# Score matmuls of 128 columns instead of 256 for the first query block of a sliding-window head

## The chip, the cores and the metric

The kernel runs on one core of one Trainium2 chip. The metric is the device time of one execution in microseconds (us). Before the change three runs took 303.61, 304.22 and 304.19 us; their median is 304.19 us. Beside them one execution was recorded by the hardware profiler; it took 303.86 us.

## The reference, cut to what matters

One decoder layer on a sequence of 512 tokens with model width 1024: a normed and modulated input is projected to queries, keys, values and gates, attention is computed for two groups of eight heads (head dimension 64, two key/value heads in each group), the results are gated, projected back and added to the input. Group a is sliding-window attention with a window of 128 keys, a relative bias and one sink per head. Group b has compressed, selected and windowed branches; the change does not touch it. Group a, in blocks of 128 queries:

```python
# query t attends keys s with 0 <= t - s < window; window = 128, blocks of 128 queries
start = i * 128
kb = keys[start - 128 : start + 128]           # zero-padded in front of key 0
dist = t[:, None] - s[None, :]
mask = (dist >= 0) & (dist < 128) & (s >= 0)
logits = einsum('btgrd,bsgd->bgrts', q_block, kb) + bias
p = masked_softmax(logits, mask, sink)
o = einsum('bgrts,bsgd->btgrd', p, v_block)
```

For the blocks i = 1, 2, 3 there are 256 keys to score. For the first block, i = 0, only the 128 keys of the block itself exist.

## The kernel before, in words

**Precision and tiles.** Everything is float32 in memory. The large products run as float32r matmuls: each operand is split into a rounded high part and a low rest, and three products (high with high, high with low, low with high) are summed in PSUM. PE stands for TensorE, DVE for VectorE, ACT for ScalarE, POOL for GpSimd.

**Stages.** Up to about 60 us of the span the input is normed, modulated and projected to the queries, keys and values of group a (`first_proj`, lines 305 to 312, tiles `sq` and `skv`). Then two strands are woven together. One is a stream of projections, `gen1` and `gen2` (lines 818 and 877), whose matmuls stand at line 513 (`unit_nat`, 256 or 280 columns) and line 524 (`unit_col`, mostly 512 columns), all into tiles `pj`. The other is a list of attention slots, run by `run` (line 1032). Its first 16 slots are of kind a, four heads r by four query blocks i, with r outermost; kind b follows. After the last slots, the output projection runs through line 524 again.

**One slot.** A slot serves two heads at a time, one for each key/value head g. It goes through four steps in four successive turns of the loop in `run`:

- `slot_scores` (line 920): for each g two float32r matmuls at line 937, with the query block as the stationary operand (128 by 128, its high and low parts stacked in the 128 rows) and the keys as the moving operand, once their high and once their low part (`hl_`). Then DVE adds the bias and takes a row minimum at line 945 (the scores are negated), POOL copies the sink into a column at line 949, and ACT takes the exponential at line 952.
- `slot_scale` (line 956): divides by the row sum, one g on DVE (line 977), one on ACT (line 975).
- `slot_trans` (line 979): PE transposes the probabilities into tiles `pt` (line 988 for up to two key blocks, line 998 for more), ACT copies them out (line 989 or 999).
- `slot_pv` (line 1003): plain float32 matmuls with the values at line 1015, gathered for all four blocks of a head.

**Widths.** In `slot_scores`, `w` is the number of keys that count: 128 for kind a with i = 0, 256 for kind a with i = 1 to 3, and 256, 384 or 512 for the slots of kind b that reach this line. `n` is the number of key columns that the matmul streams. It is `max(w, 256)`, so that it differs from `w` only for kind a with i = 0. There the matmul also scores keys 128 to 255, and nothing reads those columns: line 945 takes `ps[g][:, 0:w]`.

**What sets the order.** DVE, ACT and PE each work through one list of instructions. The list is laid out when the program is built, not by the order of the source alone. `block()` (line 531) chains the PE instructions of attention steps to one another, so that they keep the order of the source among themselves; matmuls of the stream can be placed between them. How much of the stream is written between two attention steps is set by costs in us that the generators yield and by `PER_A` (line 31).

**Other matmuls that the prediction reads.** Line 248 (`mod_col`) multiplies a 128 by 128 stationary operand with one column. Line 677 (in `cmp_mlp`) multiplies a 128 by 128 stationary operand with 64 columns, line 644 a stationary operand of 64 columns with 256 columns; all three are plain float32, and in the profile each plain float32 matmul of the source appears as two MATMULs with a LDWEIGHTS each. A float32r matmul and a transpose appear as one of each.

Of the kernel before, what the change touches and what calls it, by code (L numbers as in the profile page):

```python
# [83 lines left out]
def hybrid_layer_kernel(ctx, tc, A, out):  # L84
# [817 lines left out]
    def slot_scores_both(sl, P):  # L902

        r = sl["id"][1]
        nm = sm.tile([128, 2, 2], F32, name="nm2", bufs=2)
        dn = sm.tile([128, 2, 2], F32, name="dn2", bufs=2)
        for g in range(2):
            ps = ps_s.tile([128, 512], F32, name="s")[:, 0:256].rearrange("p (b k) -> p b k", b=2)
            for hl_ in range(2):
                PE.matmul(ps, qs[8 + 4 * g + r][:, 0:128], kTb[g][:, :, hl_, 0:128], start=hl_ == 0, stop=hl_ == 1)  # L910
            for b in range(2):
                DVE.tensor_tensor_reduce(out=P[:, g, 128 * b:128 * b + 128], in0=ps[:, b], in1=bias["b", r, g][:, 384:512],
                                         scale=1.0, scalar=3e38, op0=OP.add, op1=OP.min, accum_out=nm[:, g, b:b + 1])
        for g in range(2):
            for b in range(2):
                v = P[:, g, 128 * b:128 * b + 128]
                ACT.activation(v, v, AF.Exp, bias=nm[:, g, b:b + 1], scale=-1.0, accum_out=dn[:, g, b:b + 1])
        sl.update(P=P, dn=dn, w=256, lo=0)

    def slot_scores(sl):  # L920
        kind, r, br, i = sl["id"]
        lo = max(0, i - 1) * 128 if kind == "a" else 0
        w = (i + 1) * 128 - lo
        P = mp.tile([128, 2, 257], F32, name="pa", bufs=3) if kind == "a" else mp.tile([128, 2, 512], F32, name="pp", bufs=3)
        if br == 3:
            slot_scores_both(sl, P)
            return
        nm = sm.tile([128, 2], F32, name="nm", bufs=4)
        dn = sm.tile([128, 2], F32, name="dn", bufs=4)
        ps_a = ps_s.tile([128, 512], F32, name="s") if kind == "a" else None  # L930
        ps = []
        for g in range(2):
            h = (0 if kind == "a" else 8) + 4 * g + r
            n = max(w, 256)
            ps.append(ps_a[:, 256 * g:256 * g + n] if kind == "a" else ps_s.tile([128, 512], F32, name="s")[:, 0:n])
            for hl_ in range(2):
                PE.matmul(ps[g], qs[h][:, 128 * i:128 * i + 128], kT[br, g][:, hl_, lo:lo + n], start=hl_ == 0,  # L937
                          stop=hl_ == 1)
        for g in range(2):
            h = (0 if kind == "a" else 8) + 4 * g + r  # L940
            if kind == "a":
                bt, init = bias["a", r][:, g, 256 - w:256], nsink[:, h:h + 1]
            else:
                bt, init = bias["b", r, g][:, 512 - w:512], 3e38
            DVE.tensor_tensor_reduce(out=P[:, g, 0:w], in0=ps[g][:, 0:w], in1=bt, scale=1.0, scalar=init,  # L945
                                     op0=OP.add, op1=OP.min, accum_out=nm[:, g:g + 1])
        e = w
        if kind == "a":
            POOL.tensor_copy(P[:, :, w:w + 1], nsink[:, r:8:4][:, :, None])
            e = w + 1  # L950
        for g in range(2):
            ACT.activation(P[:, g, 0:e], P[:, g, 0:e], AF.Exp, bias=nm[:, g:g + 1], scale=-1.0,  # L952
                           accum_out=dn[:, g:g + 1])
        sl.update(P=P, dn=dn, w=w, lo=lo)
# [77 lines left out]
    def run(slots, stream):  # L1032
# [3 lines left out]
        for t in range(n + 3):  # L1036
            per = PER_A if t < 16 else PER_B[t - 16 >= PER_B[2]]
            if t < n:
                kind, r, br, i = slots[t]["id"]
                if kind == "a" and i == 0 and r >= 2:  # L1040
                    load_bias_b(r - 2)
            if 0 <= t - 2 < n:
                with block():
                    slot_trans(slots[t - 2])
            if 0 <= t - 1 < n:
                slot_scale(slots[t - 1])
            if t < n:
                with block():
                    slot_scores(slots[t])
            stream.adv(per / 2)  # L1050
            if 0 <= t - 3 < n:
                group.append(slots[t - 3])
                kind, r, br, i = slots[t - 3]["id"]
                if i == NB - 1 and (kind == "a" or br == 2):
                    with block():
                        for sl in group:
                            slot_pv(sl)
                        if jobs:
                            jobs.pop(0)()
                            stream.debt += 3.6  # L1060
                    group = []
                    if kind == "b" and br == 2 and r + 2 < 4:
                        load_bias_b(r + 2)
            stream.adv(per / 2)
# [126 lines left out]
```

## Time and profile before

| | |
|---|---|
| median of 3 runs | 304.19 us (303.61 to 304.22) |
| profiled execution, its own time | 303.86 us |
| its span, first to last instruction | 301.8 us |
| time around the span | 2.1 us |
| granted TensorE clock, mean | 1.000 |
| PE busy | 295.1 us, 98% of the span |
| weight loads (PEld) busy | 251.9 us, 83% |
| DVE busy | 238.5 us, 79% |
| ACT busy | 195.9 us, 65% |
| POOL busy | 5.2 us, 2% |

In the profile, a group is named by line, engine and operation, then "output tile <- input tiles". PE is the matmul side of TensorE and PEld its weight load; the two overlap. Ends of matmuls are modelled, so the duration of one matmul (some 0.28 us for 256 columns) is longer than the distance from its start to the start of the next. This distance, the pitch, is what a matmul costs in a run of them. Where a view merges x4 equal instructions into one row, the row gives the time from the first start to the last end; the pitch is that time less one duration, divided by three.

### The profile page before, as it was taken

What the parts mean: (1) busy time and instruction counts of PE and PEld (TensorE: products, weight loads), DVE (VectorE), ACT (ScalarE), POOL (GpSimd) and SP (SyncE); (2) the same over time, 40 slices, a digit from 0 to 9 for tenths busy, and PEclk for the clock granted to TensorE, in tenths of its full rate; (3) what the DMA queues carried; (4) which work ended last, traced back from release to release, by engine and by line L of the source; (5) the groups of instructions that cost most, each with busy time, mean ns of one, the idle gap of its engine ahead of it and who ended that gap; (6) DMA issues with size and microseconds to landing.
All of it is one profiled execution on the core that took longest, in us unless ns stands there. A gap on an engine that the chain in (4) does not pass through costs nothing.

```text
span 301.8 us, 5849 instructions
## 1 busy us (share of the span) xinstructions
PE 295.1 (98%) x2118; PEld 251.9 (83%) x2119; DVE 238.5 (79%) x668; ACT 195.9 (65%) x474; POOL 5.2 (2%) x26
## 2 busy tenths in 40 slices
PE   8899999999999999999999999999999999999995
PEld 4677888889989999999786887798888888788885
DVE  3889996999995488878999999998986867727321
ACT  4876547767976478968696665866876875723100
POOL 1000000000100000000000000000000000000000
PEclk9999999999999999999999999999999999999999
DMA  7999957993285770320770022472130000005522
GB/s 274 370 383 405 362 188 256 261 266 136 74 206 176 228 230 2 106 71 0 262 261 3 2 95 98 157 275 72 34 109 2 0 2 1 2 0 169 181 70 72
DMA packets 27420, 44.21 MB, mean 147 GB/s; under 512 B 1712, under 2 KB 19408, under 8 KB 27392
## 3 DMA queue, kind: packets, MB, share of 16 engines
q1 hardware_dynamic: 27392, 43.84, 43.3%
q8 instruction: 17, 0.28, 0.4%
q14 instruction: 11, 0.09, 0.1%
HBM read 41.70 MB, written 2.14 MB: 145 GB/s over the span
## 4 chain that ended last, share of the span: by engine, by line
PE 80%; DVE 11%; ACT 5%; DMA 2%; issue 2%; SPq 0%; ACTq 0%; DVEq 0%
PE pj L524 30%; PE sq L310 8%; PE po L1015 8%; PE s L937 7%; PE pj L513 6%; PE pt L998 4%; PE skv L311 4%; PE pt L988 3%; PE s L644 2%; DMA xf<-in_xn 2%; DVE wl L192 2%; PE s L524 2%; DVE qs L577 2%; DVE pa L945 1%; ACT pa L952 1%
## 5 line engine op out<-in xcount | busy, mean ns | idle before, releaser
L191 ACT ACTIVATE wh<-raw 128x512 fp32r<-128x512 f32 (+1 forms) x52 | 31.7, 632 | 18.7 <-PE pj L524 16.0
L192 DVE TENSOR_TENSOR wl<-raw,wh 128x512 fp32r<-128x512 f32 (+1 forms) x52 | 35.1, 692 | 3.7 <-ACT wh L191 1.8
L513 PE MATMUL pj<-wl,hh 128*128 128x256 f32 (+1 forms) x128 | 36.8, 287 | 0.0
L513 PE MATMUL pj<-wh,hh 128*128 128x256 f32 (+1 forms) x128 | 36.6, 287 | 0.0
L513 PE MATMUL pj<-wh,hl 128*128 128x256 f32 (+1 forms) x128 | 36.3, 285 | 0.0
L952 ACT ACTIVATE pp<-pp,nm 128x256 f32<-128x256 f32 (+2 forms) x48 | 29.3, 612 | 9.2 <-DVE nm L945 9.1
L524 PE MATMUL pj<-hh,wh 128*128 128x512 f32 x80 | 32.1, 402 | 0.0
L524 PE MATMUL pj<-hl,wh 128*128 128x512 f32 x80 | 31.8, 397 | 0.0
L524 PE MATMUL pj<-hh,wl 128*128 128x512 f32 x80 | 31.8, 397 | 0.0
L945 DVE CUSTOM_DVE_ANT_0 pp<-s,bias 128x256 f32<-128x256 f32 (+2 forms) x48 | 25.7, 551 | 3.5 <-PE s L937 3.3
L1015 PE MATMUL po<-ptT,xf 128*64 128x128 f32 x432 | 25.3, 274 | 0.0
L1015 PEld LDWEIGHTS po<-ptT,xf 128*64 128x64 f32 x432 | 23.5, 137 | 1.5 <-issue 0.7
L513 PEld LDWEIGHTS pj<-wl,hh 128*128 128x128 f32 x128 | 24.1, 189 | 0.2 <-issue 0.2
L513 PEld LDWEIGHTS pj<-wh,hl 128*128 128x128 f32 x128 | 24.0, 188 | 0.3 <-issue 0.3
L513 PEld LDWEIGHTS pj<-wh,hh 128*128 128x128 f32 x128 | 24.0, 188 | 0.2 <-issue 0.2
L524 PE MATMUL pj<-yl,wh 128*128 128x512 f32 (+1 forms) x64 | 23.8, 371 | 0.0
L524 PE MATMUL pj<-yh,wl 128*128 128x512 f32 (+1 forms) x64 | 23.5, 366 | 0.0
L524 PE MATMUL pj<-yh,wh 128*128 128x512 f32 (+1 forms) x64 | 23.4, 370 | 0.0
L937 PE MATMUL s<-kTb,qs 128*128 128x256 f32 (+2 forms) x96 | 23.3, 358 | 0.0
L973 DVE TENSOR_SCALAR pp<-pp,rr,xf 128x256 f32<-128x256 f32 (+2 forms) x48 | 21.1, 475 | 0.4
L999 ACT COPY ptT<-pt 128x384 f32<-128x384 f32 (+1 forms) x32 | 16.3, 527 | 6.1 <-PE pt L998 5.0
L952 ACT ACTIVATE pa<-pa,nm 128x257 f32<-128x257 f32 (+1 forms) x32 | 15.2, 477 | 4.4 <-DVE nm L945 4.3
(248 smaller groups left out, 685.1 us busy)
## 6 DMA issues: line engine op xcount, KB each, us to landing
ada_ring<-in_w_ada_ss SPq DMA_DIRECT2D x16, 512.0 KB, 9.8
raw<-in_w_cmp SPq DMA_DIRECT2D x8, 512.0 KB, 3.7
raw<-in_w_gate SPq DMA_DIRECT2D x8, 512.0 KB, 5.9
raw<-in_w_o SPq DMA_DIRECT2D x8, 512.0 KB, 3.7
wst_ring<-in_w_qkv_a SPq DMA_DIRECT2D x8, 384.0 KB, 9.4
xr<-in_xT SPq DMA_DIRECT2D x8, 256.0 KB, 2.8
bias<-line_d SPq DMA_DIRECT2D x8, 256.0 KB, 5.4
raw<-in_w_q_b SPq DMA_DIRECT2D x4, 512.0 KB, 3.6
```

Of the source, the lines that this page charges most:

```text
L191: ACT.activation(wh, src, AF.Copy)
L192: DVE.tensor_tensor(wl, src, wh.bitcast(F32), op=OP.subtract)
L310: PE.matmul(pj_q[tb], lt, w[:, 0:512], start=f, stop=l, skip_group_check=True)
L311: PE.matmul(pj_kv[tb // 2][:, tb % 2, :], lt, w[:, 512:768], start=f and tb % 2 == 0, stop=l, skip_group_check=True)
L513: PE.matmul(bank[:, t * n:(t + 1) * n], h[:, tb * 128:(tb + 1) * 128], w[:, k % 2, :], start=k == 0 and m == 0, stop=k == 7 and m == 2)
L524: PE.matmul(bank, w, h[:, cols], start=k == 0 and m == 0, stop=k == 7 and m == 2)
L937: PE.matmul(ps[g], qs[h][:, 128 * i:128 * i + 128], kT[br, g][:, hl_, lo:lo + n], start=hl_ == 0, stop=hl_ == 1)
L945: DVE.tensor_tensor_reduce(out=P[:, g, 0:w], in0=ps[g][:, 0:w], in1=bt, scale=1.0, scalar=init, op0=OP.add, op1=OP.min, accum_out=nm[:, g: ...
L952: ACT.activation(P[:, g, 0:e], P[:, g, 0:e], AF.Exp, bias=nm[:, g:g + 1], scale=-1.0, accum_out=dn[:, g:g + 1])
L973: DVE.tensor_scalar(v, v, rr[:, g:g + 1], gates[:, g, br:br + 1], op0=OP.mult, op1=OP.mult)
L999: ACT.copy(T[:, 0:nb, :], rev(pt[:, 0:nb * 128].rearrange("p (b q) -> p b q", b=nb)))
L1015: PE.matmul(o[64 * g:64 * g + 64, 128 * i:128 * i + 128], vb[:, 64 * g:64 * g + 64], sl["T"][g][:, b, :], start=first_of and b == 0, stop= ...
```

## The change

For kind a with i = 0 the matmuls at line 937 stream the 128 columns that count instead of 256. Four heads, two g and two `hl_` make 16 matmuls of the kernel's 2118 MATMULs. All other widths are as before, since `max(w, 256)` was `w` for them. Where the scores land in PSUM does not move: g = 0 starts at column 0 and g = 1 at column 256 of the same tile.

```diff
         for g in range(2):
             h = (0 if kind == "a" else 8) + 4 * g + r
-            n = max(w, 256)
+            n = w
             ps.append(ps_a[:, 256 * g:256 * g + n] if kind == "a" else ps_s.tile([128, 512], F32, name="s")[:, 0:n])
             for hl_ in range(2):
                 PE.matmul(ps[g], qs[h][:, 128 * i:128 * i + 128], kT[br, g][:, hl_, lo:lo + n], start=hl_ == 0,
```

## The prediction

> **What bounds the kernel now.** I read the page first: how busy each engine is, the span in slices, and the chain that ended last.
>
> ```profile
> span 301.8 us, 5849 instructions
> PE 295.1 (98%) x2118; PEld 251.9 (83%) x2119; DVE 238.5 (79%) x668; ACT 195.9 (65%) x474; POOL 5.2 (2%) x26
> PE   8899999999999999999999999999999999999995
> PEclk9999999999999999999999999999999999999999
> PE 80%; DVE 11%; ACT 5%; DMA 2%; issue 2%; SPq 0%; ACTq 0%; DVEq 0%
> ```
>
> PE is occupied in every slice, at the full granted clock, and carries 80% of the chain. A busy PE can still be waiting for its pipeline, so 98% alone proves little; the pitch of its matmuls says more. The second view was therefore the groups by line with shapes kept apart, and the third PE in order of time around the slots concerned, for one of them (kind a, r = 2, i = 0) from 109 us.
>
> ```profile
> L937 PE MATMUL s<-kT,qs 128*128 128x256 f32 x64 | 12.0, 304 | 0.1
> ```
>
> ```profile
> 107.15 0.28 PE L513 MATMUL pj<-wh,hh 128*128 128x256 f32 x1
> 107.27 0.28 PE L513 MATMUL pj<-wl,hh 128*128 128x256 f32 x1
> 107.39 0.28 PE L513 MATMUL pj<-wh,hl 128*128 128x256 f32 x1
> ...
> 108.77 0.60 PE L988 MATMUL pt<-xf,pa 128*128 128x128 f32 x4
> 109.12 0.72 PE L937 MATMUL s<-kT,qs 128*128 128x256 f32 x4
> ```
>
> ```profile
> 109.09 0.54 PEld L937 LDWEIGHTS s<-kT,qs 128*128 128x128 f32 x4
> 109.56 0.31 PEld L802 LDWEIGHTS pt<-xf 128*128 128x128 f32 x2
> ```
>
> All kind-a scores are one group of 64 matmuls of 256 columns; a quarter of them, 16, belong to i = 0. The stream's 256-column matmuls start every 0.12 us: 0.24 over two steps, 107.15 to 107.39. The score group's weight loads run from 109.09 to the next load at 109.56, so four score matmuls take 0.47 us, 0.118 each, the stream's pitch. PE goes straight on to other matmuls before and after. So a change in their pitch passes on to the end almost whole, and the question is what pitch a float32r matmul of 128 columns has. The trace has none under 256 columns. The answer lies between rows of other kinds.
>
> **What is taken away: columns.** What does a column cost? The rows before the first score matmul show 512 and 256 columns side by side.
>
> ```profile
> 62.47 0.39 PE L524 MATMUL pj<-hl,wh 128*128 128x512 f32 x1
> 62.69 0.39 PE L524 MATMUL pj<-hh,wl 128*128 128x512 f32 x1
> 62.92 0.28 PE L513 MATMUL pj<-wh,hh 128*128 128x256 f32 x1
> 63.04 0.28 PE L513 MATMUL pj<-wl,hh 128*128 128x256 f32 x1
> ...
> 64.28 0.35 PE L937 MATMUL s<-kT,qs 128*128 128x256 f32 x1
> ...
> 65.64 0.38 PE L937 MATMUL s<-kT,qs 128*128 128x256 f32 x1
> ...
> 68.37 0.39 PE L937 MATMUL s<-kT,qs 128*128 128x256 f32 x1
> ...
> 69.54 0.75 PE L937 MATMUL s<-kT,qs 128*128 128x256 f32 x5
> ```
>
> From 62.47 to 62.92 two matmuls of 512 columns take 0.225 us each; the next, of 256, takes 0.12 us. So 256 columns more cost 0.107 us and 128 columns 0.053 us. If columns alone set the pitch, it would fall from 0.118 to 0.065 us, and 16 matmuls would save 16 x 0.053 = 0.85 us. That is the lower end.
>
> **What stays: the weight load.** Each of the 16 matmuls still loads 128 by 128 weights. What does PE do when the columns are so few that the load must show? Two groups tell.
>
> ```profile
> 12.81 0.52 PEld L248 LDWEIGHTS pj<-ones,macc 128*128 128x128 f32 x4
> ```
>
> ```profile
> 101.87 0.52 PEld L677 LDWEIGHTS s<-xf,csT 128*128 128x128 f32 x4 [0.18 <-ACT csT L670]
> ```
>
> ```profile
> L248 PEld LDWEIGHTS pj<-ones,macc x8: 186/190/192, 12.8 to 19.0; 128*128 128x128 f32 x8
> L248 PE MATMUL pj<-ones,macc x8: 164/250/250, 12.8 to 19.0; 128*128 128x1 f32 x8
> ```
>
> At line 248 each matmul streams one column, at line 677 it streams 64. Yet both times four loads take 0.52 us from first start to last end. Less one load of 0.190, that is 0.33 us over three steps: a pitch of 0.110 us, with one column as with 64. The load sets it. These are plain float32, but their load is the same as that of the scores: 0.190 us here, and (0.54 - 3 x 0.118) = 0.19 us in the score group. So I take 0.110 us as the pitch of a 128-column score matmul. The saving is (0.118 - 0.110) x 16 = 0.13 us. At 256 columns the stream and the load are nearly level; beneath that, fewer columns only uncover the load.
>
> The Trainium skill speaks for the lower end: its page "TensorE: Matmul & The Clock Gate", section "Back-to-back issue gap", gives N/2.4 + 2.5 ns for a warm matmul of N columns, 56 ns for 128, and 81 ns for 128 columns in a stream of load and matmul pairs. By 56 ns the 16 matmuls would save an estimated 1.0 us, by 81 ns 0.6 us. The trace's 0.110 us with a single column speaks against both for this load, so I keep them as a rival only.
>
> **What the scores release.** A shorter last matmul also ends up to 0.053 us earlier. Does DVE wait for it? Of the scores' releases, the line's own view and DVE in order of time say:
>
> ```profile
>   DVE pa L945: 1.2, 2
> ```
>
> ```profile
> 69.18 0.69 DVE L634 TENSOR_TENSOR pp<-cmpt,xf 128x512 f32<-128x512 f32 x1
> 69.91 0.35 DVE L945 CUSTOM_DVE_ANT_0 pa<-s,bias,nsink 128x128 f32<-128x128 f32 x1
> ```
>
> ```profile
> 109.76 0.48 DVE L945 CUSTOM_DVE_ANT_0 pa<-s,bias,nsink 128x256 f32<-128x256 f32 x1
> 110.16 0.34 DVE L945 CUSTOM_DVE_ANT_0 pa<-s,bias,nsink 128x128 f32<-128x128 f32 x1
> ```
>
> DVE waited twice for kind-a scores, and neither 128-wide step shown carries a wait: each follows another DVE step at once. At 110.16 the scores had been done since 109.84 (109.12 + 0.72). So an earlier end is worth nothing there, and DVE's own steps were 128 wide already. Nothing is added: no wait, no transfer, no PSUM tile. POOL and the DMA queues keep their lists. The cover of this zero is DVE's own backlog; without it the worth is at most 4 x 0.053 = 0.2 us.
>
> **The sum.** Against the profiled execution: 303.86 - 0.13 = 303.73 us. This execution lies 0.33 us below the median of the three runs, inside their spread. Against the median it is 304.06. I predict 304.0. A difference under 0.2%, 0.6 us, is about what a measurement of this kernel cannot tell from none, so this forecast means no change.
>
> **Rival 1: columns set the pitch after all.** If PE takes the load of the next weights further ahead than line 248 lets it show, the pitch falls to 0.065 us, and the saving is the 0.85 us above: 303.3 us. For it: 0.225 for 512 and 0.118 for 256 lie on the straight line that columns alone would draw, so the load has not shown itself in a float32r group yet. Against it: at line 248 one column leaves a load all the room there is, and the pitch stays at 0.110. Chance 0.10.
>
> **Rival 2: a narrow float32r matmul loses its single fast pass.** This is the case on the other side. What does plain float32 cost here, that float32r escapes?
>
> ```profile
> L644 PE MATMUL s<-raw,pp x64: 379/379/493, 91.2 to 99.6; 128*64 128x256 f32 x64
> ```
>
> ```profile
> L1015 PE MATMUL po<-ptT,xf x80: 272/273/323, 264.0 to 268.3; 128*64 128x128 f32 x80
> ```
>
> For 128 columns more, one pass of plain float32 lasts 379 - 273 = 106 ns longer; float32r pays 53 ns. And plain float32 needs two passes. So 128 columns cost 2 x 0.106 = 0.21 us in streaming; by line 677's loads, two passes cost 2 x 0.110 = 0.22 us. If the fast float32r pass needs a certain width, as the row of the 64 score matmuls cannot exclude, since none of them is narrower than 256, then the 16 matmuls cost 16 x (0.22 - 0.118) = 1.63 us more: 305.5 us against the profiled time, 305.8 against the median. PE has no idle time at the slots to take that up. It decides from a pitch of 0.118 + 0.61/16 = 0.156 us upward. For it: every float32r matmul in the trace has 256 columns or more, so the trace holds nothing against it but the equal weight load. Against it: float32r shows as one MATMUL with one load at each width from 256 to 512, on one straight law; nothing in the trace announces a step. Chance 0.25.
>
> **Rival 3: PE's list is laid out anew.** The first slot's four score matmuls are written as one run. In the rows above they start at 64.28, 65.64, 68.37 and within the five from 69.54, with stream matmuls between. So something lays out the list ahead of the chip, and if it counts columns, the narrower matmuls may shift what stands between attention steps. What a shift is worth I bound by waits of weight loads for such steps:
>
> ```profile
> PEld pt L570 <- PE pj L524: 0.8, 1, 0.8
> ...
> PEld s L937 <- ACT kT L595: 0.3, 1, 0.3
> ```
>
> One such wait more or fewer is 0.3 to 0.8 us, two of them up to 1.2 us, in either direction: 302.9 to 305.3 around 304.06. For it: the scattered order. Against it: only 16 of 2118 matmuls change, by little. Chance 0.18, of which 0.08 is faster and 0.10 slower by over 0.6 us.
>
> That the change does less than it says I leave out: the width stands in every row of the group, and no other slot has w under 256.
>
> **How the numbers follow.** The forecast has 0.47, rival 1 0.10, rival 2 0.25, rival 3 0.18. Faster by over 0.2%: 0.10 + 0.08 = 0.18. Slower: 0.25 + 0.10 = 0.35. Within: 0.47. The forecast's own range is 303.5 to 304.6, the spread of the runs around 304.06 with a little of the weaving. For 8 in 10 the range must take in rival 1 (303.3), rival 2 (305.8, and a tenth or two for the spread) and most of rival 3: 303.0 to 306.0.
>
> **What the changed profile would show.** In the group of line 937 with tile `kT`, 16 matmuls carry 128x128 and 48 carry 128x256. Right: in the runs of four narrow score matmuls, the loads take 0.52 us from first start to last end, pitch 0.110, and the next load follows within 0.44 to 0.47 us of the first. Rival 1: that run shrinks to 0.39 us. Rival 2: the run grows to about 0.85 us, or 32 MATMULs stand where 16 did. Rival 3: the pitch is 0.110 but the time differs, and the rows between two attention steps, or the first slot's scatter, are not the same. The forecast is wrong if the pitch of the narrow matmuls lies above 0.156 us or if the time moves by more than 0.6 us with the pitch as said.

## The result and the profile after

The changed kernel takes 306.28 us (median of 4 runs, 306.17 to 306.46); the kernel before took 304.12 us beside it (4 runs, 303.61 to 304.22). The ratio is 1.0079, with a 95% interval of 1.0067 to 1.0091: slower by 2.2 us, and above the predicted range. The profiled execution of the changed kernel took 306.46 us.

The page of the changed kernel, its first lines and its chain:

```profile
span 304.7 us, 5848 instructions
PE 295.8 (97%) x2118; PEld 252.0 (83%) x2119; DVE 238.7 (78%) x668; ACT 196.4 (64%) x474; POOL 5.2 (2%) x26
PEclk9999999999999999999999999999999999999999
...
PE 75%; DVE 11%; ACT 7%; DMA 3%; issue 2%; SPq 1%; DVEq 0%; ACTq 0%
```

Every engine has about the work that it had before, and the clock is full. The span is 2.9 us longer, and PE's part of the chain fell from 80 to 75%: more of the chain runs through other engines. Next, whether the matmuls behaved. The groups by line with shapes apart, and the weight loads in order of time around one narrow run:

```profile
L937 PE MATMUL s<-kT,qs 128*128 128x256 f32 x48 | 8.6, 302 | 0.0
L937 PE MATMUL s<-kT,qs 128*128 128x128 f32 x16 | 3.1, 285 | 0.1
```

```profile
73.44 0.20 PEld L988 LDWEIGHTS pt<-xf,pa 128*128 128x128 f32 x2 [0.48 <-ACT pa L975]
...
86.59 0.49 PEld L988 LDWEIGHTS pt<-xf,pa 128*128 128x128 f32 x4 [0.96 <-ACT pa L952]
...
108.13 0.53 PEld L937 LDWEIGHTS s<-kT,qs 128*128 128x128 f32 x4
108.58 0.19 PEld L513 LDWEIGHTS pj<-wh,hl 128*128 128x128 f32 x1
...
112.97 0.30 PEld L802 LDWEIGHTS pt<-xf 128*128 128x128 f32 x2 [0.75 <-DVE xf L800]
...
118.56 0.42 PEld L590 LDWEIGHTS pt<-xf,kn 128*128 128x128 f32 x4 [0.52 <-DVE kn L585]
...
127.46 0.19 PEld L513 LDWEIGHTS pj<-wl,hh 128*128 128x128 f32 x1 [0.47 <-DVE wl L192]
```

The four narrow scores at 108.13 load in 0.53 us, a pitch of (0.53 - 0.19) / 3 = 0.113 us, and the next load follows after 0.45 us. That is as predicted. The brackets in the other rows are the news: the weight loads wait 0.47 to 0.96 us in front of transposes and projections whose input ACT or DVE has not finished. Before, none of the steps at lines 802, 590 (118 us) and 513 (127 us) waited.

Where does the lost time lie? A window over the stretch from the first kind-a score to the start of the last kind-a run of four, the kernel before and then after (span of the window, then busy time of PE, PEld, DVE, ACT and POOL with instruction counts, clock, DMA share, GB/s):

```profile
64.28:141.64 77.36, 76.79 (x671) 73.47 (x671) 62.04 (x196) 59.66 (x158) 3.52 (x13) 1.00 0.43 131
```

```profile
64.84:144.44 79.60, 77.10 (x672) 73.25 (x671) 62.18 (x196) 60.14 (x158) 3.55 (x13) 1.00 0.43 128
```

This stretch grew by 2.24 us. PE's busy time in it grew by 0.31; the time in which PE does nothing grew from 0.57 to 2.50 us, by 1.93. So nearly all of the loss is PE waiting between first and last kind-a score, with the same work on every engine. From there to the end both kernels take the same time. (The first score is 0.56 us later in this one execution; in the kernel `wide_new_list` below, which has the same lists, it starts at 64.30 us as before, so that part is not the change.)

PE's own idle time stands in front of the same five steps. After, and then the one such row of before:

```profile
73.47 0.41 PE L988 MATMUL pt<-xf,pa 128*128 128x128 f32 x2 [0.30 <-DVE pa L977]
...
86.62 0.70 PE L988 MATMUL pt<-xf,pa 128*128 128x128 f32 x4 [0.76 <-DVE rr L969]
...
112.98 0.46 PE L802 MATMUL pt<-xf 128*128 128x96 f32 x2 [0.54 <-DVE xf L800]
...
118.56 0.66 PE L590 MATMUL pt<-xf,kn 128*128 128x128 f32 x4 [0.31 <-DVE kn L585]
...
127.46 0.39 PE L513 MATMUL pj<-wl,hh 128*128 128x256 f32 x1 [0.26 <-DVE wl L192]
```

```profile
85.86 0.71 PE L988 MATMUL pt<-xf,pa 128*128 128x128 f32 x4 [0.27 <-DVE pa L977]
```

That is 2.17 us against 0.27, and the difference of 1.90 us is nearly all of the 1.93. (The brackets of the weight loads are longer: part of each wait lies under the row of the matmul before it.)

One wait followed to its cause: line 802 at 112.97 waits for DVE line 800, which waits for ACT line 799. ACT in order of time, after:

```profile
109.83 0.19 ACT L952 ACTIVATION_READ_ACCUMULATOR pa<-pa,nm 128x1 f32 x1
109.92 0.62 ACT L191 ACTIVATE wh<-raw 128x512 fp32r<-128x512 f32 x1
110.45 0.49 ACT L975 ACTIVATE pa<-pa,rr 128x256 f32<-128x256 f32 x1
110.84 0.39 ACT L952 ACTIVATE pa<-pa,nm 128x129 f32<-128x129 f32 x1
111.14 0.19 ACT L952 ACTIVATION_READ_ACCUMULATOR pa<-pa,nm 128x1 f32 x1
111.23 0.39 ACT L952 ACTIVATE pa<-pa,nm 128x129 f32<-128x129 f32 x1
111.53 0.19 ACT L952 ACTIVATION_READ_ACCUMULATOR pa<-pa,nm 128x1 f32 x1
111.62 0.25 ACT L838 ACTIVATE xf<-pj 128x128 f32<-128x128 f32 x1
...
112.41 0.27 ACT L799 ACTIVATE xf<-xf 128x96 f32<-128x96 f32 x1
```

and before:

```profile
106.45 0.26 ACT L838 ACTIVATE xf<-pj 128x128 f32<-128x128 f32 x1
...
107.93 0.28 ACT L799 ACTIVATE xf<-xf 128x96 f32<-128x96 f32 x1
```

After, ACT takes four exponentials (line 952), a weight split (line 191) and a scaling (line 975) first and reaches line 838 only at 111.62. Before, it had passed line 799 when PE came to line 802 at 109.56. No instruction became slower; they stand in another order.

How much, the order of the instructions in the two traces says. Counted in stream matmuls (lines 513 and 524) that stand ahead of an attention step in PE's list:

```
step on PE               before  after  difference
scores by L644, L644        206    201     -5
L677, L680                  218    213     -5
L697 and two slots after    255    236    -19
L802                        255    266    +11
next slot's transposes      273    266     -7
L590, L1015                 292    299     +7
next slot and all later     309    309      0
```

In the traces PE's order has another weight load at 205 of 2119 places (from 65 to 119 us of the kernel before), DVE's another instruction at 64 of 668 and ACT's at 37 of 474 (76 to 129 us), POOL's at none. SP's list differs too, in 5 of 110 places as the lists are written in the experiments below. So the edit did two things: it narrowed 16 matmuls, and it let the whole stretch around them be laid out anew. My theory at this point: the second is the whole loss. Its rivals: the narrow matmuls cost something where the trace does not show it, or both have a part.

### The profile page after: what moved, and what is told of

It is laid out like the page before. It is cut to its first block, busy times and chain, and to the rows that moved or that the text cites. A ratio compares the mean times of both kernels' runs of the same rounds, so it can differ in the third digit from the quotient of the medians.

```text
span 304.7 us, 5848 instructions
## 1 busy us (share of the span) xinstructions
PE 295.8 (97%) x2118; PEld 252.0 (83%) x2119; DVE 238.7 (78%) x668; ACT 196.4 (64%) x474; POOL 5.2 (2%) x26
## 4 chain that ended last, share of the span: by engine, by line
PE 75%; DVE 11%; ACT 7%; DMA 3%; issue 2%; SPq 1%; DVEq 0%; ACTq 0%
PE pj L524 29%; PE sq L310 8%; PE po L1015 7%; PE s L937 6%; PE pt L998 4%; PE skv L311 4%; PE pj L513 3%; DMA ada_ring<-in_w_ada_ss 3%; PE pt L988 3%; PE s L644 2%; ACT pa L952 2%; DVE pa L945 2%; DVE wl L192 2%; PE s L524 2%; DVE qs L577 1%
```

## The experiments

The lists can be held. A function at the end of the kernel chains each engine's instructions in a written order, without adding a wait; `PIN` is the order wanted. In the traces of `narrow_old_list` and `wide_new_list` PE, DVE, ACT and POOL then run in the order of before and of the changed kernel, instruction by instruction.

```diff
+    pin(tc)
...
+def pin(tc):
+    at = {i.name: i for i in tc.nc.cur_bb.bb.instructions}
+    info = mybir.DependencyInfo(mybir.DependencyClass.NoSync, mybir.DependencyReason.DATA)
+    for listed in PIN.values():
...
+        for a, b in zip(names, names[1:]):
+            tc.add_manual_dep(at[b], a, info, reason="pin")
```

**Width and order apart: two kernels.** `narrow_old_list` is the changed kernel with before's lists; `wide_new_list` has before's 256 columns and the lists of the changed kernel.

> The 16 narrow matmuls of the change, but every engine's list of instructions held in the order that it had before the change. Theory A (the lists that the build laid out anew cost the time, the narrow matmuls themselves save a little): 303.9 to 304.2 us, and the narrow matmuls at a pitch of 0.110 us. Theory B (the narrow float32r matmuls themselves cost the time, or upset what runs beside them): 306 us, as after the change.

> The 16 matmuls at 256 columns as before the change, but every engine's list held in the order that it has after the change. Theory A: 306.2 to 306.5 us, all of the loss without a narrow matmul. Theory B: 304.1 us, as before.

`narrow_old_list`: 303.81 us against 303.65, ratio 1.0004 (0.9996 to 1.0013). `wide_new_list`: 306.00 us, ratio 1.0075 (1.0062 to 1.0088). Both lie 0.1 to 0.2 us under the range that theory A gave and far from theory B; the kernel before, too, took less here than the 304.12 us of the first measurement. The rows of `narrow_old_list`, line 937 and the same stretch in a window:

```profile
L937 PE MATMUL s<-kT,qs x64: 223/282/367, 64.4 to 142.2; 128*128 128x256 f32 x48, 128*128 128x128 f32 x16
```

```profile
64.42:141.78 77.36, 76.72 (x673) 73.38 (x671) 62.05 (x196) 59.69 (x158) 3.43 (x13) 1.00 0.45 132
```

and of `wide_new_list`, the window:

```profile
64.30:143.83 79.53, 77.13 (x671) 73.35 (x671) 62.23 (x196) 60.12 (x158) 3.60 (x13) 1.00 0.43 128
```

With 16 narrow matmuls in the old order the last run of four starts at 141.77, so the stretch takes 77.35 us, what it took before. With no narrow matmul in the new order it takes 79.53. The order is the loss, and the width is worth nothing that can be measured.

**Which part of the stretch.** Lists changed over at line 680, about 102 us: the new order up to there and the old one behind (`new_then_old`), and the reverse (`old_then_new`).

```diff
-PIN = after's lists
+PIN = after's lists up to line 680, the rest in before's order
```

> Narrow matmuls; the lists are those after the change up to the small matmuls of line 680, about 103 us into the span, and from there the order from before. If the loss lies in the late part (lines 697 to 1015, where attention steps come 19 stream matmuls earlier and line 802 comes 11 later): 304.0 to 304.5 us. If it lies in the early part, where steps come 1 to 5 stream matmuls earlier: 305.5 to 306.3.

> Narrow matmuls; the lists from before the change up to line 680, and from there the order after it. If the loss lies in the late part: 305.7 to 306.3 us. If it lies in the early part: 304.0 to 304.5.

304.34 us, ratio 1.0030 (1.0019 to 1.0041), and 305.48 us, ratio 1.0063 (1.0051 to 1.0075), against 303.65. By the ratios both parts lose, the early one some 0.9 us and the late one some 1.9; together somewhat more than the whole. I had expected one part to carry it. It is not one spot.

**The pitch by itself.** 120 float32r matmuls appended at the end of the kernel (their result is not used): 24 each of 256, 192, 128 and 64 columns, then 12 pairs of 512 and 128.

```diff
+        for widths in ((256,), (192,), (128,), (64,), (512, 128)):
+            bank = PJ()
+            for m in range(24):
+                n = widths[m % len(widths)]
+                PE.matmul(bank[:, 0:n], hh[m % 8][:, 128 * (m // 8):128 * (m // 8) + 128], hl[m % 8][:, 0:n],
+                          start=True, stop=True)
```

> The changed kernel with 120 float32r matmuls added behind its last one, each with a weight load of its own: 24 of 256 columns, 24 of 192, 24 of 128, 24 of 64, then 512 and 128 in turn, 24 in all. If the weight load sets a floor: pitch 0.118, 0.110, 0.110, 0.110 us, and 0.33 to 0.335 us for a pair of 512 and 128. If columns alone set it: 0.118, 0.091, 0.065, 0.038 and 0.29 for a pair. If float32r under 256 columns falls to two passes: 0.118, then 0.32, 0.22, 0.22 or more. The time grows by what they take, some 15 us.

Weight loads of the appended line in four windows of the timeline, inside the groups of 256, 192, 128 and 64 columns in turn, and the pairs as one group:

```profile
300.56 2.82 PEld L1127 LDWEIGHTS pj<-hl,hh 128*128 128x128 f32 x23
...
303.43 2.54 PEld L1127 LDWEIGHTS pj<-hl,hh 128*128 128x128 f32 x22
...
306.12 2.42 PEld L1127 LDWEIGHTS pj<-hl,hh 128*128 128x128 f32 x21
...
308.91 2.20 PEld L1127 LDWEIGHTS pj<-hl,hh 128*128 128x128 f32 x19
```

```profile
L1127 PEld LDWEIGHTS pj<-hl,hh x24: 187/191/192, 311.5 to 315.4; 128*128 128x128 f32 x24
```

Less one load of 0.19 us, and divided by one step less than there are loads, the pitches are 0.120, 0.112, 0.112 and 0.112 us. At these widths under 256 the width no longer matters: the load sets the pitch. A pair of 512 and 128 takes 3.9 us / 11.5 = 0.34 us, as much as 0.225 for the wide one and 0.112 for the narrow one, so a long matmul ahead does not hide more of the next load. The answer is read from the pitches; the total, 318.45 us, is a single run and is not used.

**A third width.** If only the order counts, 192 columns, which the pitch cannot tell from 128, may give any time.

```diff
-            n = w
+            n = max(w, 192)
```

> The 16 matmuls at 192 columns, the lists left to the build, which lays them out in a third way. Theory A (only the list counts): pitch of the 16 matmuls 0.110 to 0.115 us, and a time that the width does not order: anywhere from 303.5 to 307, not half way between before and after except by chance. Theory B (each column less costs in proportion): half way, 304.9 us.

307.94 us against 303.96, ratio 1.0131 (1.0117 to 1.0145): slower than both neighbours. Its list is a third one, with attention steps up to 31 stream matmuls away from before's. The time of these three widths does not follow the width:

```profile
L937 PE MATMUL s<-kT,qs x64: 272/282/366, 64.6 to 145.6; 128*128 128x256 f32 x48, 128*128 128x192 f32 x16
```

**Some of the sixteen.** Narrow matmuls for r = 0 alone, r = 1 alone, r = 2 and 3, with the lists that the build then lays out.

```diff
-            n = w
+            n = w if r == 0 else max(w, 256)
```

> Only the first of the four heads (r = 0) narrow, lists left to the build. Against the list before, attention steps stand up to 6 stream matmuls earlier (19 with the whole change). If the displacement on the lists sets the loss: 304.3 to 305.0 us, a fraction of the whole. If each narrow matmul carries a share of the loss: a quarter of 2.2 us, 304.5 us, and the same for only_r1 and half for only_r23.

> Only the second head (r = 1) narrow, lists left to the build: nothing moves before r = 1, then up to 7 stream matmuls. Displacement: 304.2 to 304.9 us. Share for each matmul: 304.5 us.

> The last two heads (r = 2 and 3) narrow, lists left to the build, which hardly change: one stretch of up to 4 stream matmuls. Displacement: 303.8 to 304.2 us, as before. Share for each matmul: half of 2.2 us, 305.1 us.

303.99, 304.39 and 304.01 us against 303.65: ratios 1.0011 (1.0002 to 1.0021), 1.0022 (1.0013 to 1.0031) and 1.0017 (1.0008 to 1.0026). The sum, 0.50%, falls short of 0.79%: the loss is no price per matmul. Attention steps are displaced by at most 7 stream matmuls here, not 19. `only_r0` and `only_r23` came out well under what a price per matmul gave (304.5 and 305.1 us), `only_r0` also under the 304.3 us expected from its displacement; `only_r1` fits both.

**Which wait.** Three attempts to take the waits of the changed kernel away, with PE's list as it is. `new_mended` moves the four ACT steps of line 802's chain, and DVE's, ahead (the numbers are lines of the kernel in the order of the list):

```diff
 ScalarE:  952 952
+          838 840 799
           191 975
+          550
           952 952
-          838
           975
-          840 799 550
```

> The changed kernel with TensorE's list untouched; on ScalarE and VectorE five steps of the last window projection (lines 838, 840, 799, 550 and 839, 800, 554) are moved ahead of the softmax steps that the new lists put before them. If the loss of the late part comes from TensorE waiting for line 800 (0.75 us) and line 585 (0.52 us) because those steps queue too late: both waits go, and the time falls by 0.8 to 1.2 us, to 304.8 to 305.2. If TensorE's own new order costs the time whatever the other engines do: 305.8 to 306.2.

306.61 us against 303.96, ratio 1.0091 (1.0078 to 1.0105). Line 802 no longer waits, and nothing is won. Its weight loads:

```profile
111.94 0.19 PEld L513 LDWEIGHTS pj<-wl,hh 128*128 128x128 f32 x1 [0.54 <-DVE wl L192]
112.75 0.31 PEld L802 LDWEIGHTS pt<-xf 128*128 128x128 f32 x2
...
118.33 0.42 PEld L590 LDWEIGHTS pt<-xf,kn 128*128 128x128 f32 x4 [0.50 <-DVE kn L585]
```

The weight split that was pushed back now arrives late, 0.8 us ahead of line 802. `new_mended2` keeps the split first, moves those four steps ahead of the next slot's exponentials only, one split (lines 191 and 192) ahead of another slot's, and the first half of the norm that line 590 needs ahead of a bias step:

```diff
 ScalarE:  191 975
-          952 952
           838
-          975
           840 799 550
+          952 952 975
 VectorE:  803 557
-          945 945
           103 104 105 106
+          945 945
```

> The changed kernel with TensorE's list untouched; ScalarE and VectorE take lines 838, 839, 840, 799, 800 and 550 only after the weight split that stood ahead of them (lines 191 and 192), so that the first mending's new wait does not arise; four steps of the norm (lines 103 to 106) move ahead of a bias step, and one weight split at 126 us ahead of a softmax. If the waits at the head of TensorE's list are the loss, and can be taken away where nothing else that TensorE needs is pushed back: the waits for lines 800 and 192 go, that for line 585 shrinks, and the time falls by 1.0 to 1.7 us against the change, to 304.5 to 305.2. If any such gain is paid back at the next wait, as in the first mending: 306.0 to 306.6.

306.40 us against 303.65, ratio 1.0096 (1.0079 to 1.0112). The waits at 802 and 513 are gone, and line 590 has them:

```profile
118.06 0.42 PEld L590 LDWEIGHTS pt<-xf,kn 128*128 128x128 f32 x4 [1.48 <-DVE kn L585]
...
150.44 0.42 PEld L570 LDWEIGHTS pt<-xf,qn 128*128 128x128 f32 x4 [1.44 <-PE pj L524]
```

The wait at line 570, too, grew, from 0.88 us in the changed kernel to 1.44.

`new_mended3` moves the rest of that norm (lines 107 to 110, 583 and 585) ahead of the same bias step too.

> The second mending, and in addition the whole norm of the window keys (lines 103 to 110, 583, 585) directly behind its sum of squares on VectorE's list, ahead of the bias steps of the next slot. If VectorE's norm chain is what TensorE meets at line 590 and the time follows from it: the wait of 1.48 us there goes or falls under 0.3 us, and the time falls to 304.7 to 305.3 us. If the time is set elsewhere: TensorE waits as long further on (lines 988 or 570), and 306.0 to 306.6 us.

307.65 us against 303.81, ratio 1.0125 (1.0110 to 1.0141): worse. ACT and the weight loads of `new_mended3`:

```profile
116.95 0.51 ACT L952 ACTIVATE pa<-pa,nm 128x257 f32<-128x257 f32 x1 [3.21 <-DVE nm L945]
```

```profile
126.43 0.19 PEld L513 LDWEIGHTS pj<-wh,hh 128*128 128x128 f32 x1 [1.25 <-ACT wh L191]
127.36 0.19 PEld L513 LDWEIGHTS pj<-wl,hh 128*128 128x128 f32 x1 [0.74 <-DVE wl L192]
```

Line 590 is served, but the bias step behind the norm came later on DVE, ACT stood still for 3.21 us waiting for its minimum, and nine microseconds on the weight splits reach PE late. That the one leads to the other is my reading; no run separates them. In all three attempts the waits that were taken away came up at other places.

**Can the old order gain?** With the narrow matmuls and before's lists, two tries to remove waits that before already had. `fewer_waits` moves five PE steps (lines 988, 937, 570 with 910, 749, 998) 2 to 4 stream matmuls later; `old_tuned` moves two DVE steps (line 554 behind line 977 at 86 us, line 192 behind line 563 at 148 us).

```diff
 TensorE:
-          988 988 937 937   513 513 513 513
+          513 513 513 513   988 988 937 937
```

> Narrow matmuls on the lists from before the change, with five steps on TensorE's list moved 2 to 4 stream matmuls later, where the profile of the narrow matmuls on the old list shows TensorE waiting 0.32, 0.42, 0.74, 0.42 and 0.41 us for them. If a wait at the head of TensorE's list is the price of an order, the five give back 1.2 to 2.0 us: 301.8 to 302.6. If later steps only push the waits on to what follows: 303.5 to 304.0.

> Narrow matmuls on the old lists, TensorE's untouched; on VectorE two steps are moved: a sum of squares (line 554) behind the scaling that TensorE waits 0.42 us for at 86 us, and a weight split (line 192) behind the query norm that TensorE waits 0.74 us for at 148 us. If such chains set the time: both waits shrink, and 302.8 to 303.4 us against 303.8. If not: 303.6 to 304.1.

304.22 us against 303.96, ratio 1.0006 (0.9997 to 1.0015), and 304.37 against 303.81, ratio 1.0021 (1.0012 to 1.0030). No gain; no version here beats the kernel before. The trace of `fewer_waits` shows what became of the waits. The five waits, 2.31 us together in `narrow_old_list`, are gone, and four others are new or longer:

```profile
73.05 0.20 PEld L988 LDWEIGHTS pt<-xf,pa 128*128 128x128 f32 x2 [0.47 <-ACT pa L975]
...
90.11 0.42 PEld L590 LDWEIGHTS pt<-xf,kn 128*128 128x128 f32 x4 [0.80 <-ACT pa L975]
...
152.36 0.42 PEld L988 LDWEIGHTS pt<-xf,pa 128*128 128x128 f32 x4 [0.65 <-issue]
...
191.65 0.30 PEld L910 LDWEIGHTS s<-kTb,qs 128*128 128x128 f32 x2 [0.74 <-DVE nm L945]
```

In `narrow_old_list` these places have 0.25 us, 0.29, no wait that the view marks, and 0.26. All waits of weight loads over 0.15 us between 60 and 250 us add up to 9.68 us there and to 9.64 in `fewer_waits`.

**Which engine's list.** The narrow matmuls, PE's new list, and the old lists of DVE, ACT and the transfers.

```diff
-PIN = {PE, DVE, ACT, SP, POOL of before}
+PIN = {PE of after; DVE, ACT, SP, POOL of before}
```

> The 16 narrow matmuls, TensorE's list of the changed kernel, but the lists of VectorE, ScalarE and the transfers of the kernel before. If the loss comes from TensorE asking in another order for what the other two deliver in the old one, it stays or grows: 306 us or more. If it comes from the new order on VectorE and ScalarE, it goes: 303.8 to 304.4 us. In between (304.8 to 305.5) both have a part. My expectation is the first, since the attention steps on TensorE stand up to 19 stream matmuls earlier while the step that they wait for is no earlier.

310.08 us (308.32 to 310.53) against 303.60, ratio 1.0205 (1.0178 to 1.0232). Three of its five executions were granted a clock of 0.994; the profiled one, at 0.999, took 308.32 us, still 4.7 us above the kernel before. So PE's new order with the others' old ones costs more than the whole change, and the new lists of the others win about half of that back. The profiled execution: the waits of weight loads, then DVE in order of time.

```profile
PEld pt L697 <- issue: 2.7, 1, 2.7
...
PEld pt L988 <- ACT pa L952: 2.2, 2, 1.5
```

```profile
107.19 0.69 DVE L192 TENSOR_TENSOR wl<-raw,wh 128x512 fp32r<-128x512 f32 x1
107.80 0.35 DVE L693 SCALAR_TENSOR_TENSOR kcn<-s,n_y,xf 128x128 f32<-128x128 f32 x1
```

PE comes to line 697 nineteen stream matmuls early and stands 2.7 us in front of it, until 108.26: DVE makes its input `kcn` at 107.80, behind four weight splits, as in the old order. The view calls the wait "issue", but the load starts 0.11 us after `kcn` is done at 108.15. In the changed kernel DVE's list takes line 693 ahead of three of these splits, at 106.26. On the other hand the wait at line 802, 0.75 us in the changed kernel, is absent here, where PE comes to it later:

```profile
113.68 0.31 PEld L802 LDWEIGHTS pt<-xf 128*128 128x128 f32 x2
```

So which waits appear depends on the lists of all engines together. The opposite mixture, PE's old list with new lists for the others, was not tried: in it the engines would wait for each other in a ring.

## Why the prediction was wrong, point by point

**The pitch** was right. Forecast: 0.110 us, next load 0.44 to 0.47 us after the first. Measured: 0.113 and 0.45 us in the changed kernel, 0.112 by itself at 192, 128 and 64 columns. The Trainium skill, page "TensorE: Matmul & The Clock Gate", section "LDWEIGHTS (loading the stationary operand)", puts a load of P columns at P/1.2 ns, for 128 an estimated 107 ns. The measured pitch of 0.112 to 0.113 us lies 5 to 6% above.

**The sum** was right for the edit itself. I took 0.13 us off; with the lists held, the change is +0.04% (-0.04 to +0.13%), that is between 0.12 us less and 0.4 us more. Within that lies "no change"; my own 0.13 us lies at its edge.

**What the scores release**, priced at nothing, was right as well: `narrow_old_list` has the stretch of before to 0.01 us.

**Rivals 1 and 2** fell. 16 MATMULs with one load each appear, at 0.113 us, neither 0.065 nor above 0.156. The Trainium skill's 81 ns for pairs of load and matmul at 128 columns, from the section "Back-to-back issue gap" of the same page, does not appear either: no group of `pitch_by_width` comes below 0.112 us.

**Rival 3 is the step that failed**: its mechanism was right, its size was wrong, and I gave it too little weight. In the sum the new order stands at nothing; `wide_new_list`, which has the new order alone, measures it at 0.75%, 2.3 us. Rival 3 read: "One such wait more or fewer is 0.3 to 0.8 us, two of them up to 1.2 us, in either direction." Measured: 2.2 us, and five waits new or longer. The rows above carry 0.48 + 0.96 + 0.75 + 0.52 + 0.47 us, 3.18 us together, against 0.24 and 0.46 us at the first two of these places before and none at the others; that is 2.5 us more for the weight loads, of which PE itself stood idle for 1.90. The other waits of the stretch changed little; one of 0.26 us, at line 570, is new. Three things were wrong in that rival.

- *Number.* I counted waits as if a new list changed one or two places. It changed the order over some 60 us (65 to 129 us of the kernel before), by up to 19 stream matmuls, which at 0.12 us are 2.3 us of PE's time.
- *Sign.* I priced gain and loss alike. Five new lists were measured with the layout that the build gave them (all sixteen narrow, 192 columns, r = 0, r = 1, r = 2 and 3), and all five come out slower, by 0.11 to 1.31%, three of them near what a measurement can tell. Why none is faster is open; five are few.
- *The weight against it.* "Only 16 of 2118 matmuls change, by little" was no argument. What is laid out anew does not shrink with the edit: 192 columns are the smaller edit and cost more than 128.

**"Nothing is added: no wait, no transfer"** took the lists as fixed, while rival 3 said that they might not be. "POOL and the DMA queues keep their lists" was right for POOL and wrong for SP, whose list differs in 5 of 110 places. What SP's share of the loss is was not measured by itself.

**The condition for being wrong** was met in its second form: the time moved by more than 0.6 us with the pitch as said. The range ended at 306.0 because of rival 2; a rival 3 sized by the number of matmuls that may move would have carried it further.

**What is shown and what stays open.** Shown: the new order makes the loss, and the width none that can be measured. Both halves of the new order lose (`new_then_old`, `old_then_new`), and PE's new list loses with the old lists of the others too (`pe_new`). Not shown: that PE's list alone is the cause, since the reverse mixture can't run, and why the build lays the lists out as it does. Not settled: a single place in the new order that could be mended. Three attempts moved the wait and did not shorten the time. In the window DVE is busy for 62 and ACT for 60 of 80 us, and both must meet PE at every slot, so a step moved ahead is likely to make another late. This, and that no small repair exists, is argued and not shown.

## What to carry to other kernels

Where the build lays out the order, changing one tile's size changes the order of everything near it: compare the built lists engine by engine before believing that an edit is local, and hold the lists fixed to see what the edit itself is worth. Price a new layout by how far it can move the steps, not by the number of instructions edited: here largest moves of 31, 19, 7, 6 and 4 stream matmuls went with losses of 1.31, 0.79, 0.22, 0.11 and 0.17%. Do not count on a gain from taking one wait away where three engines meet at every step; five tries here brought none. Where the load sets a matmul's pitch, fewer columns buy nothing: here 64, 128 and 192 columns cost the same, and 256 under 0.01 us more.

## What the runs showed of the hardware that was not expected

- A float32r matmul with its own 128 by 128 load keeps one pitch, 0.112 us, at 64, 128 and 192 columns; 256 columns cost 0.120. A 512-column matmul ahead of it does not shorten it: the pair takes 0.34 us.
- The same granted clock went with different losses. In `pe_new` three executions with a mean granted clock of 0.994 have spans of 307.7 to 308.3 us, two with 0.999 have 306.2 and 306.4; in `new_mended3` one with 0.994 has 305.9 us, and three with 0.998 to 1.000 have 305.4 to 305.7. What lowers the granted clock, and whether it accounts for the difference, no trace shows, since both profiled executions were at 0.999 or above.
